# The first products after two inner norms run on unnormalised activations, with rstd and the shift applied to their sums

## The chip, the cores and the metric

The kernel runs on one core of one Trainium2 chip. The metric is the device time of one execution in microseconds (us), taken as the median of several runs; lower is better. TensorE (PE in the profile) multiplies matrices, VectorE (DVE), ScalarE (ACT) and GpSimd (POOL) do elementwise work, and SyncE (SP) issues the transfers from HBM. Each engine works through its own queue in order and waits on semaphores for the others.

## The reference

One decoder layer for 256 tokens of width 2048, all in float32. Each of three sublayers first normalises x and modulates it with a scale and a shift computed from a condition c:

```python
def ada_in(x, g, shift, scale):
    y = rmsnorm(x, g) * (1.0 + scale[:, None, :]) + shift[:, None, :]
    return y
...
    mod = cond @ ada_w[l] + ada_b[l]
    sh1, sc1, gt1, sh2, sc2, gt2, sh3, sc3, gt3 = jnp.split(mod, N_MOD, axis=-1)
    h = ada_in(x, norm_g[l, 0], sh1, sc1)
    x = x + MACARON_W * gt1[:, None, :] * swiglu(h, ffn_w_gate[l, 0], ffn_w_up[l, 0], ffn_w_down[l, 0])
    h = ada_in(x, norm_g[l, 1], sh2, sc2)
    x = x + gt2[:, None, :] * hybrid_mixer(h, ...)
    h = ada_in(x, norm_g[l, 2], sh3, sc3)
    x = x + MACARON_W * gt3[:, None, :] * swiglu(h, ffn_w_gate[l, 1], ffn_w_up[l, 1], ffn_w_down[l, 1])
return rmsnorm(x, final_norm)
```

rmsnorm divides each token's vector by the root of its mean square: one factor rstd for each token. swiglu has 5632 hidden units (44 tiles of 128, called f). hybrid_mixer projects h to eight heads of forgetting attention (q, k, v), to q, k, v, z of eight heads of a gated delta rule, and to 24 gate rows; the delta rule's q, k and v go through a causal convolution of four taps and a silu, and its keys into a triangular solve.

## The kernel before

x lies feature-major in SBUF, as 16 blocks j (or k) of 128 features by 256 tokens. The weights stream from HBM in blocks of eight 128x128 tiles (512 KB). For each block `Stream.next` (L85 to L106) issues a DMA into `wraw`, has ScalarE cast the high half `whi` (L95) and VectorE subtract it to get the low half `wlo` (L98, the "low split"); three buffers of each rotate, and a fourth during the ffns. Both operands of every product are so split in two, and three partial products stand for one float32 product. `mm` (L360) does a tile in two matmuls: the high weights on high and low activations side by side (512 columns), the low weights on the high activations (256 columns). The mixer's `project` uses three matmuls of 256 columns (L614 to L616).

The modulated activations are `hs`, [128, 16, 2, 256], high and low beside each other for each k. The columns of `mod` (shift, scale and gate of the three sublayers) are computed along the way: `ada_col` (L193) loads 1 MB and reduces it on VectorE (L214, tile `adat`). The table `RATE` says how many of them go with each weight block; `W.quiet` stops them for the last three j of an ffn's second half.

The stages run one after another: ffn0, the mixer, ffn1, the final norm. An ffn runs in two halves of its f tiles; each half computes gate and up products (`pg`, `pu`, summed over k), silu and product (`hid`), and then for each of the 16 blocks j the down products `pd`. `residual` (L385, L386) adds a block's sum to x, in two VectorE steps: one for each half of the 512 columns, scaled by the gate column `gh` (L383). In the second half `sumsq_add` squares the new block on ScalarE (`sq`, L257) and adds it up on GpSimd (`sqacc`, L261). The mixer ends in the out projection, which does the same with sums called `po`: four blocks at once, then one after the other.

The norm stands between two stages. `norm_rstd` sums the squares over the partitions (`nsum`, L269), takes root and reciprocal in small steps (L274 to L279), and spreads rstd into a row that lies on all partitions (`rb` L283, `nrow` L284). Then `modulate_one` makes a block of `hs`: x times g(1 + scale) times the row (`ht`, L297), plus the shift, rounded to the high half on ScalarE and subtracted to the low half on VectorE (L299 to L304). `h_need(k)` has four blocks made ahead of the product that reads block k. ffn1 starts with a group of two f (four sums) that runs over k in the outer loop; the mixer's first stage has the gate rows `gt` and three key heads (four sums), also with k outside.

In the mixer, `ORDER` sets the sequence of the projections: K is a key head, Z and V rows for four heads at once (`project_rows`, L627 to L629), G a delta-rule head's q and v, F an attention head. Convolutions (`cv`, L763 to L765), gates (L656 to L698) and the solve are generators whose steps are taken between product tiles, and `finish` forces what a later step needs. Within the order in which the program is written, a scheduler places the instructions of each engine.

## Time and profile before

| | us |
|---|---|
| median of 3 runs | 2083.11 |
| lowest, highest run | 2080.29, 2083.84 |
| the profiled execution | 2078.41 |
| its span in the trace | 2076.6 |
| VectorE, low splits (674 of 1228 ns) | 823.6 |
| ScalarE, casts of the high halves (674 of 1048 ns) | 701.8 |
| VectorE, ada columns (140 of 2352 ns) | 329.3 |

The mean clock that TensorE was granted in the profiled execution is 0.988. A row of a timeline reads: start and duration, engine, line, operation, output from inputs, shape, count; a bracket at its end gives the idle time of that engine before it, and what ended it. A row of a group reads: line, engine, operation, names, shapes and count, then busy time and the mean of one in ns, then the idle time before them and what ended it. Several matmuls are in flight at once, so a matmul's own duration is longer than the distance to the next.

### The profile page before, as it was taken

The numbers are of one execution on the slowest core, as the hardware profiler recorded it, in microseconds if no ns is written. First come the engines' busy times: TensorE is split into PE (matmuls) and PEld (weight loads), VectorE is DVE, ScalarE is ACT, GpSimd is POOL, SyncE is SP. The second block draws the span as 40 slices with busy tenths as digits, with TensorE's granted clock in tenths as the row PEclk, the third lists the DMA queues.
The fourth block names the chain that finished last, engine by engine and source line by source line (L and its number), as shares of the span: only waits on it lengthen the run. The fifth ranks groups of instructions, "written<-read, shape, count | busy, mean of one in ns | idle before, by whom it ended". The sixth has DMA issues, their size and how long they took to land.

```text
span 2076.6 us, 33353 instructions
## 1 busy us (share of the span) xinstructions
PE 2029.3 (98%) x12965; PEld 1825.4 (88%) x12966; DVE 1559.8 (75%) x2386; ACT 1012.5 (49%) x1577; POOL 66.8 (3%) x60
## 2 busy tenths in 40 slices
...
GB/s 312 349 326 323 279 208 255 360 339 368 333 328 326 330 304 182 236 251 231 206 258 224 197 241 281 205 231 231 240 234 213 185 190 184 191 184 189 187 184 110
DMA packets 129488, 519.55 MB, mean 250 GB/s; under 512 B 18217, under 2 KB 21545, under 8 KB 111153
## 3 DMA queue, kind: packets, MB, share of 16 engines
...
q8 instruction: 102, 1.67, 0.3%
...
## 4 chain that ended last, share of the span: by engine, by line
PE 87%; DVE 6%; DMA 2%; ACT 2%; issue 1%; DVEq 0%; SPq 0%; ACTq 0%
PE pd L361 15%; PE pu L361 11%; PE pg L361 11%; PE pd L362 8%; PE pg L362 5%; PE pu L362 5%; PE pgu L431 5%; PE pgu L429 5%; PE pgu L430 5%; PE po L361 3%; PE pp L614 2%; PE pp L616 2%; PE pp L615 2%; DVE wlo L98 2%; PE po L362 1%
## 5 line engine op out<-in xcount | busy, mean ns | idle before, releaser
L98 DVE TENSOR_TENSOR wlo<-wraw,whi 128x1024 fp32r<-128x1024 f32 x674 | 823.6, 1228 | 348.7 <-ACT whi L95 346.4
L95 ACT CAST whi<-wraw 128x1024 fp32r<-128x1024 f32 x674 | 701.8, 1048 | 685.5 <-issue 171.0
L361 PE MATMUL pd<-hid,whi 128*128 128x512 f32 x1408 | 497.0, 397 | 0.0
L362 PE MATMUL pd<-hid,wlo 128*128 128x256 f32 x1408 | 396.0, 281 | 0.8 <-DVE wlo L98 0.7
L361 PE MATMUL pg<-hs,whi 128*128 128x512 f32 x960 | 342.5, 397 | 2.3 <-DVE hs L304 1.8
L361 PE MATMUL pu<-hs,whi 128*128 128x512 f32 x960 | 343.2, 398 | 0.0
L214 DVE CUSTOM_DVE_ANT_0 adat<-adat,cs,colt 128x2048 f32<-128x2048 f32 x140 | 329.3, 2352 | 16.5 <-DMA adat<-in_ada_dram 16.1
L361 PEld LDWEIGHTS pd<-hid,whi 128*128 128x128 f32 x1408 | 264.2, 188 | 64.7
L362 PE MATMUL pg<-hs,wlo 128*128 128x256 f32 x960 | 270.6, 282 | 0.0
L362 PE MATMUL pu<-hs,wlo 128*128 128x256 f32 x960 | 270.2, 281 | 0.0
L362 PEld LDWEIGHTS pd<-hid,wlo 128*128 128x128 f32 x1408 | 265.4, 189 | 2.5 <-DVE wlo L98 2.1
L429 PE MATMUL pgu<-hs,whi 128*128 128x256 f32 x896 | 251.4, 283 | 5.2 <-ACT hs L300 4.0
L431 PE MATMUL pgu<-hs,wlo 128*128 128x256 f32 x896 | 250.7, 284 | 2.4 <-DVE wlo L98 2.3
L430 PE MATMUL pgu<-hs,whi 128*128 128x256 f32 x896 | 252.2, 283 | 0.0
L361 PEld LDWEIGHTS pg<-hs,whi 128*128 128x128 f32 x960 | 181.0, 188 | 45.8 <-issue 2.1
L361 PEld LDWEIGHTS pu<-hs,whi 128*128 128x128 f32 x960 | 180.9, 188 | 43.9
L614 PE MATMUL pp<-hs,whi 128*128 128x256 f32 x656 | 191.9, 294 | 4.0 <-ACT whi L95 2.1
L616 PE MATMUL pp<-hs,wlo 128*128 128x256 f32 x656 | 188.9, 289 | 0.5 <-DVE wlo L98 0.4
L615 PE MATMUL pp<-hs,whi 128*128 128x256 f32 x656 | 188.3, 287 | 0.0
L362 PEld LDWEIGHTS pg<-hs,wlo 128*128 128x128 f32 x960 | 181.9, 190 | 0.0
L362 PEld LDWEIGHTS pu<-hs,wlo 128*128 128x128 f32 x960 | 181.9, 189 | 0.0
L429 PEld LDWEIGHTS pgu<-hs,whi 128*128 128x128 f32 x896 | 171.0, 192 | 6.3 <-ACT hs L300 4.4
...
## 6 DMA issues: line engine op xcount, KB each, us to landing
wraw<-in_w_dram SPq DMA_DIRECT2D x674, 512.0 KB, 4.2
adat<-in_ada_dram SPq DMA_DIRECT2D x140, 1024.0 KB, 6.6
...
```

The source lines that it names most:

```text
L95: nc.scalar.copy(self.h, r)
L98: nc.vector.tensor_tensor(self.l, r, self.h.bitcast(F32), ALU.subtract)
L214: V.tensor_tensor_reduce(t, t, cs, 1.0, L("adab", q, 1), ALU.mult, ALU.add, mod[:, q : q + 1])
L361: PE.matmul(ps, wt[0], act.rearrange("p a t -> p (a t)"), start=first, stop=False)
L362: PE.matmul(ps[:, :T], wt[1], act[:, 0], start=False, stop=last)
L429: PE.matmul(o, wh, hs[:, k, 0], start=first and s == 0, stop=False, skip_group_check=skip)
L430: PE.matmul(o, wh, hs[:, k, 1], start=False, stop=False, skip_group_check=skip)
L431: PE.matmul(o, wl, hs[:, k, 0], start=False, stop=last, skip_group_check=skip)
L614: PE.matmul(pp[i][:, :T], wh, hs[:, k, 0], start=(k == 0), stop=False)
L615: PE.matmul(pp[i][:, :T], wh, hs[:, k, 1], start=False, stop=False)
L616: PE.matmul(pp[i][:, :T], wl, hs[:, k, 0], start=False, stop=(k == KD - 1))
```

## The change

Since rstd is one factor for each token, it can be multiplied into a product's sum after the fact: W(x g (1 + scale) rstd + shift) = rstd W(x g (1 + scale)) + W shift.

- `hs` gets a flat layout of 514 columns for each k: low half, high half, and two columns with the high and low half of the shift.
- A class `Early` stands for a norm. `y(j)`, called after each residual of ffn0's second half and of the out projection, takes the gain g(1 + scale) of block j (`g1`, VectorE), writes its product with x as the high half (ScalarE, L334) and the low half (VectorE, L335). `norm1` is that of the mixer, `norm2` that of ffn1.
- `products` does a tile in three matmuls: the high weights on the high half and the shift (258 columns), the high weights on the low half (256), the low weights on the high half and the shift (258).
- `step(k)` puts the sum of the squares at k = 2 and the row at k = 4 of the first products; the row is copied to SBUF. From then on `modulate_one` writes the finished blocks over `hs`, behind the products that read it.
- `scaled` finishes a sum: the two shift columns are added, the sum is multiplied by the row, and the shift's product is handed on as a bias for the next step.
- The mixer's first stage now holds the gate rows and five key heads (six sums), ffn1's first group three f (six sums). `ORDER` has V0 ahead of G0, and V0 finishes the chain of keys up to head 0.
- `W.quiet` and the rules that held VectorE's low splits and ada columns behind the norm (`W.held`, `W.hold` from `norm_rstd`) are gone.
- Products on finished blocks use `mm_h`, the same two matmuls as `mm`.

```diff
+N_EARLY = 5
...
-ORDER = ("K3 K4 K5 K6 K7 Z0 G0 V0 F0 G1 F1 G2 F2 G3 F3 V1 Z1 G4 F4 G5 F5 G6 G7 F6 F7").split()
+ORDER = ("K5 K6 K7 Z0 V0 G0 F0 G1 F1 G2 F2 G3 F3 V1 Z1 G4 F4 G5 F5 G6 G7 F6 F7").split()
...
-    def norm_rstd(keep_row=False):
+    def norm_sums():
...
+        for t in range(2):
+            V.tensor_scalar(rb[:, t], L("ones"), y[:, t : t + 1], None, ALU.mult)
+        return rb
+    def norm_row(rb, eng):
         pr = psf("nrow")
         for t in range(2):
-            last = V.tensor_scalar(rb[:, t], L("ones"), y[:, t : t + 1], None, ALU.mult)
             PE.matmul(pr[:, t * P : (t + 1) * P], rb[:, t], ident, start=True, stop=True)
-        W.held = ([None, sqa["hold"]] if sqa["hold"] is not None else []) + [last.ins]
-        if not keep_row:
-            return pr[:, :T]
         row = tmp.tile([P, T], F32, name="nrow", bufs=1)
-        V.tensor_copy(row, pr[:, :T])
+        eng(row, pr[:, :T])
         return row
-    hs = keep.tile([P, KD, 2, T], F32R, name="hs")
+    hs = keep.tile([P, KD, 2 * T + 2], F32R, name="hs")
+    LO, HI, HIS, ALL = slice(0, T), slice(T, 2 * T), slice(T, 2 * T + 2), slice(0, 2 * T)
...
-    def modulate(which, m_sh, m_sc):
-        ada_need(max(m_sh, m_sc), KD - 1)
-        g1 = gains(which, m_sc, 0, KD)
-        r = norm_rstd()
-        hq["next"], hq["one"] = 0, lambda j: modulate_one(
-            j, g1[:, j : j + 1], mod[:, m_sh * KD + j : m_sh * KD + j + 1], r)
+    class Early:
+        def __init__(self, which, m_sh, m_sc):
+            self.which, self.m_sh, self.m_sc, self.row, self.sums = which, m_sh, m_sc, None, None
+        def y(self, j):
+            ada_need(self.m_sc, j)
+            ada_need(self.m_sh, KD - 1)
+            if j == 0:
+                sh = mod[:, self.m_sh * KD : (self.m_sh + 1) * KD]
+                A.copy(hs[:, :, 2 * T], sh)
+                V.tensor_sub(hs[:, :, 2 * T + 1], sh, hs[:, :, 2 * T].bitcast(F32))
+            g = gains(self.which, self.m_sc, j, 1)
+            A.activation(hs[:, j, HI], x[:, j], AF.Copy, scale=g)
+            V.scalar_tensor_tensor(hs[:, j, LO], x[:, j], g, hs[:, j, HI].bitcast(F32), ALU.mult, ALU.subtract)
+        def step(self, k):
+            if k == 2:
+                self.sums = norm_sums()
+            if k == 4:
+                self.row = norm_row(self.sums, A.copy)
+                g1 = gains(self.which, self.m_sc, 0, KD)
+                hq["next"], hq["one"] = 0, lambda j: modulate_one(
+                    j, g1[:, j : j + 1], mod[:, self.m_sh * KD + j : self.m_sh * KD + j + 1], self.row)
+            if k > 4:
+                h_upto(min(k, k - 4 + max(0, k - 10)))
+        def products(self, ps, wt, k):
+            PE.matmul(ps[:, : T + 2], wt[0], hs[:, k, HIS], start=(k == 0), stop=False)
+            PE.matmul(ps[:, :T], wt[0], hs[:, k, LO], start=False, stop=False)
+            PE.matmul(ps[:, : T + 2], wt[1], hs[:, k, HIS], start=False, stop=(k == KD - 1))
+        def scaled(self, dst, ps, rows=slice(0, P)):
+            s = tiny.tile([P, 2], F32, name="shc", tag="shc", bufs=8)
+            A.copy(s[rows, :1], ps[rows, T : T + 1])
+            V.tensor_add(s[rows, 1:], ps[rows, T + 1 : T + 2], s[rows, :1])
+            V.tensor_tensor(dst, ps[rows, :T], self.row[rows], ALU.mult)
+            return s[rows, 1:]
...
-        while hq["next"] < min(KD, k + AHEAD):
+        h_upto(k + AHEAD)
+    def h_upto(n):
+        while hq["next"] < min(KD, n):
...
+    def mm_h(ps, wt, k):
+        PE.matmul(ps, wt[0], hs[:, k, ALL], start=(k == 0), stop=False)
+        PE.matmul(ps[:, T:], wt[1], hs[:, k, HI], start=False, stop=(k == KD - 1))
...
+            first = early is not None and len(grp) > 1
+            for i, (f, m, k) in enumerate(todo):
+                if first:
+                    if i % (2 * len(grp)) == 0:
+                        early.step(k)
+                    early.products(pg[f, m], W.next((m, which), k, f), k)
+                else:
+                    h_need(k)
+                    mm_h(pg[f, m], W.next((m, which), k, f), k)
...
+                if first:
+                    sg, su = early.scaled(tg, pg[f, "g"]), early.scaled(tu, pg[f, "u"])
+                    A.activation(tg, tg, AF.Silu, bias=sg)
+                    V.scalar_tensor_tensor(tu, tu, su, tg, ALU.add, ALU.mult)
+                    hd = hp.tile([P, 2, T], F32R, name="hid", tag="hid")
+                    split(hd, tu)
+                    hids.append(hd)
...
-                    if half == 0:
-                        modulate(2 * which, m_sh, m_sc)
-                    hids = gate_up(which, part, 2 if half == 0 else 1, hp)
+                    hids = gate_up(which, part, 3 if half == 0 else 1, hp, early if half == 0 else None)
...
                     if half == 1:
                         sumsq_add(j)
-                        if j == KD - 4:
-                            W.quiet = True
+                        if after is not None:
+                            after.y(j)
                         if j == KD // 2:
                             sqrt_table(x[:, j, :1])
-                W.quiet = False
...
+    norm1, norm2 = Early(1, 3, 4), Early(2, 6, 7)
     if dbg is None or "ffn1" in dbg:
-        ffn(0, 0, 1, 2)
+        ffn(0, 2, None, norm1)
...
         def gates(ps):
             yr = x[:, 8]
-            A.copy(yr[R], ps[R])
+            sh = norm1.scaled(yr[R], ps, R)
+            A.activation(yr[R], yr[R], AF.Identity, bias=sh)
...
-                if h:
-                    finish("k", NH)
+                finish("k", NH if h else 0)
...
-        first = project([("gt", 0)] + [("qkv", NH + h) for h in range(3)])
-        start("k", -1, gates(first[0]))
-        for h in range(3):
-            have_keys(h, first[1 + h])
+        first = [("gt", 0)] + [("qkv", NH + h) for h in range(N_EARLY)]
+        pp = [psn(i, "pp") for i in range(len(first))]
+        for k in range(KD):
+            norm1.step(k)
+            for i, (m, n) in enumerate(first):
+                norm1.products(pp[i], W.next(m, k, n), k)
+        h_upto(KD)
+        start("k", -1, gates(pp[0]))
+        for h in range(N_EARLY):
+            v = pt("v")
+            sh = norm1.scaled(v, pp[1 + h])
+            A.activation(v, v, AF.Identity, bias=sh)
+            have_keys(h, v)
...
                 residual(pj[q], j, 5, False)
                 sumsq_add(j)
+                norm2.y(j)
...
-        ffn(1, 6, 7, 8)
+        ffn(1, 8, norm2)
```

Three places show how instructions move. The first is TensorE at norm 1, between the last down product of ffn0 (`pd`) and the first of the mixer (`pp`). Before:

```order
L362 MATMUL pd_8121<-hid_7307,wlo_8147 128x256
L269 MATMUL nsum_8177<-colt_87,sqacc_7362 128x2 [waits Pool_49]
L269 MATMUL nsum_8177<-colt_87,sqacc_7362 128x2
L269 MATMUL nsum_8177<-colt_87,sq_8170 128x2 [waits Activation_49]
L269 MATMUL nsum_8177<-colt_87,sq_8170 128x2
L284 MATMUL nrow_8192<-colt_87,rb_8191 128x128 [waits DVE_49] x2
L614 MATMUL pp_8245<-hs_126,whi_8269 128x256 [waits PE_49,Activation_49]
L614 MATMUL pp_8246<-hs_126,whi_8269 128x256 [waits PE_49]
L614 MATMUL pp_8247<-hs_126,whi_8269 128x256 [waits PE_49]
```

After:

```order
L411 MATMUL pd_8186<-hid_7307,wlo_8215 128x256
L270 MATMUL nsum_8349<-colt_87,sqacc_7362 128x2 [waits Pool_49]
L270 MATMUL nsum_8349<-colt_87,sqacc_7362 128x2
L270 MATMUL nsum_8349<-colt_87,sq_8238 128x2 [waits Activation_49]
L270 MATMUL nsum_8349<-colt_87,sq_8238 128x2
L350 MATMUL pp_8295<-hs_126,whi_8303 128x258 [waits Activation_49]
L351 MATMUL pp_8295<-hs_126,whi_8303 128x256
L350 MATMUL pp_8296<-hs_126,whi_8303 128x258 [waits DVE_49,PE_49]
L351 MATMUL pp_8296<-hs_126,whi_8303 128x256
```

and some rows on:

```order
L351 MATMUL pp_8298<-hs_126,whi_8303 128x256
L350 MATMUL pp_8299<-hs_126,whi_8303 128x258
L351 MATMUL pp_8299<-hs_126,whi_8303 128x256
L350 MATMUL pp_8300<-hs_126,whi_8303 128x258
L352 MATMUL pp_8295<-hs_126,wlo_8304 128x258 [waits DVE_49]
```

The row's two matmuls have left this place; the first product waits for ScalarE alone, and the high weights of the first block go to five sums twice and to the sixth once before a low weight is used. The row stands 72 products later.

The second place is TensorE at norm 2, from the last product of the out projection (`po`) on; before, the sum and the row stood directly behind it, as at norm 1. After, there come first the products, then behind 36 of them the sum,

```order
L411 MATMUL po_14324<-oh_13573,wlo_14350 128x256
L350 MATMUL pg_14391<-hs_126,whi_14399 128x258 [waits Activation_49]
L351 MATMUL pg_14391<-hs_126,whi_14399 128x256
L352 MATMUL pg_14391<-hs_126,wlo_14400 128x258 [waits DVE_49]
L350 MATMUL pu_14392<-hs_126,whi_14399 128x258 [waits DVE_49,PE_49]
```

```order
L352 MATMUL pu_14396<-hs_126,wlo_14430 128x258
L270 MATMUL nsum_14445<-colt_87,sqacc_13675 128x2 [waits Pool_49]
L270 MATMUL nsum_14445<-colt_87,sqacc_13675 128x2
L270 MATMUL nsum_14445<-colt_87,sq_14371 128x2 [waits Activation_49]
L270 MATMUL nsum_14445<-colt_87,sq_14371 128x2
```

and behind 36 more the row:

```order
L352 MATMUL pu_14396<-hs_126,wlo_14477 128x258
L290 MATMUL nrow_14504<-colt_87,rb_14459 128x128 [waits DVE_49] x2
L350 MATMUL pg_14391<-hs_126,whi_14513 128x258
L351 MATMUL pg_14391<-hs_126,whi_14513 128x256
L352 MATMUL pg_14391<-hs_126,wlo_14514 128x258
```

What stood between `po` and `pg` stands between products now.

The third place is VectorE in the down products of ffn0's second half, from one residual to the next but one. Before:

```order
L385 SCALAR_TENSOR_TENSOR x_85<-pd_7581,gh_7626,x_85 128x256
L98 TENSOR_TENSOR wlo_7662<-wraw_7659,whi_7661 128x1024
L386 SCALAR_TENSOR_TENSOR x_85<-pd_7581,gh_7626,x_85 128x256
L98 TENSOR_TENSOR wlo_7692<-wraw_7689,whi_7691 128x1024
L383 TENSOR_SCALAR gh_7736<-mod_125 128x1
L98 TENSOR_TENSOR wlo_7714<-wraw_7711,whi_7713 128x1024
L385 SCALAR_TENSOR_TENSOR x_85<-pd_7633,gh_7681,x_85 128x256
L386 SCALAR_TENSOR_TENSOR x_85<-pd_7633,gh_7681,x_85 128x256
L214 ISA adat_7717,mod_125<-adat_7717,cs_86,colt_87 128x2048
L214 ISA mod_125 128x1
L383 TENSOR_SCALAR gh_7791<-mod_125 128x1
L98 TENSOR_TENSOR wlo_7747<-wraw_7744,whi_7746 128x1024
```

After:

```order
L434 SCALAR_TENSOR_TENSOR x_85<-pd_7603,gh_7648,x_85 128x256
L99 TENSOR_TENSOR wlo_7688<-wraw_7685,whi_7687 128x1024
L435 SCALAR_TENSOR_TENSOR x_85<-pd_7603,gh_7648,x_85 128x256
L99 TENSOR_TENSOR wlo_7722<-wraw_7719,whi_7721 128x1024
L335 SCALAR_TENSOR_TENSOR hs_126<-x_85,g1_7655,hs_126 128x256
L432 TENSOR_SCALAR gh_7766<-mod_125 128x1
L315 SCALAR_TENSOR_TENSOR g1_7773<-mod_125,colt_87 128x1
L99 TENSOR_TENSOR wlo_7744<-wraw_7741,whi_7743 128x1024
L434 SCALAR_TENSOR_TENSOR x_85<-pd_7659,gh_7707,x_85 128x256
L435 SCALAR_TENSOR_TENSOR x_85<-pd_7659,gh_7707,x_85 128x256
L215 ISA adat_7747,mod_125<-adat_7747,cs_86,colt_87 128x2048
L215 ISA mod_125 128x1
```

For each block there is one step more on `hs` and one more on `g1`, with ada column and low splits around them.

Behind the end of the mixer's first stage VectorE now begins with the convolutions of five key heads and their six scalings, where it had the convolutions of three. Up to the low split of Z0's first block those of K0 to K5 stand there in both kernels; the step that starts the solve's matrix (`Ln`, from `cstt`) and most of K6's convolution, which stood ahead of that split, come behind it.

43 lines of the change are left out of this document (20 added, 23 removed).

## Prediction

> **What bounds the kernel now.** I began with the page's first two lists, which give the busy share of each engine over the whole span, and then the chain that ended last.
>
> ```profile
> span 2076.6 us, 33353 instructions
> PE 2029.3 (98%) x12965; PEld 1825.4 (88%) x12966; DVE 1559.8 (75%) x2386; ACT 1012.5 (49%) x1577; POOL 66.8 (3%) x60
> PE 87%; DVE 6%; DMA 2%; ACT 2%; issue 1%; DVEq 0%; SPq 0%; ACTq 0%
> ```
>
> TensorE is busy for 98% of the span, so the kernel is bound by matmuls, and what can be won is the time in which TensorE stands or runs at half clock. The profiled execution took 2078.41 us, 1.8 above its span; the median of the runs shown is 2083.11, 4.7 above that execution. Differences worked out below from the trace are taken off the median.
>
> The next view is the timeline around the second inner norm (before ffn1). These are TensorE's rows from the last product of the out projection to the first of ffn1.
>
> ```profile
> 1305.89 0.28 PE L362 MATMUL po<-oh,wlo 128*128 128x256 f32 x1
> 1306.01 0.57 PE L269 MATMUL nsum<-colt,sqacc 128*128 128x2 f32 x4
> ...
> 1307.77 0.61 PE L269 MATMUL nsum<-colt,sq 128*128 128x2 f32 x4 [1.19 <-ACT sq L257]
> ...
> 1309.91 1.22 PE L284 MATMUL nrow<-colt,rb 128*128 128x128 f32 x4 [1.53 <-DVE rb L283]
> ...
> 1312.98 0.76 PE L361 MATMUL pg<-hs,whi 128*128 128x512 f32 x1 [1.84 <-DVE hs L304]
> ```
>
> Each bracket is a wait for another engine: the square of the last block, the rstd row, the first modulated block. From 1306.17 to 1312.98 no product runs: 6.81 us. The first norm (before the mixer) has the same shape:
>
> ```profile
> 787.66 0.28 PE L362 MATMUL pd<-hid,wlo 128*128 128x256 f32 x1
> ...
> 789.08 0.42 ACT L257 ACTIVATE sq<-x 128x256 f32<-128x256 f32 x1 [1.99 <-DVE x L386]
> ...
> 791.68 0.71 PE L284 MATMUL nrow<-colt,rb 128*128 128x128 f32 x4 [1.53 <-DVE rb L283]
> ...
> 793.95 1.22 PE L614 MATMUL pp<-hs,whi 128*128 128x256 f32 x4 [1.55 <-ACT hs L303]
> ```
>
> From 787.94 to 793.95 it is 6.01 us. A table of windows shows that the gaps cost more than their length (columns: window, length, busy time of each engine with its count, then granted clock, DMA share and GB/s):
>
> ```profile
> 200.00:320.00 120.00, 120.00 (x1009) 120.00 (x1008) 98.07 (x148) 59.02 (x86) 0.00 (x0) 1.00 0.71 250
> 787.70:794.00 6.30, 1.96 (x15) 1.59 (x13) 5.47 (x14) 1.29 (x4) 1.32 (x5) 0.93 0.59 209
> 794.00:800.00 6.00, 6.00 (x28) 6.00 (x29) 4.35 (x12) 3.13 (x7) 0.42 (x2) 0.51 0.27 87
> 800.00:802.00 2.00, 2.00 (x19) 2.00 (x18) 1.67 (x3) 2.00 (x6) 0.00 (x0) 1.00 0.00 0
> 1313.00:1319.00 6.00, 6.00 (x19) 5.13 (x20) 4.78 (x11) 2.93 (x6) 0.00 (x0) 0.52 0.16 54
> 1400.00:1700.00 300.00, 300.00 (x1705) 261.12 (x1704) 186.26 (x233) 130.49 (x170) 0.00 (x0) 1.00 0.63 216
> ```
>
> For some 6 us after each gap the clock is 0.51 and 0.52. At full clock a 256-column matmul takes 120/1009 = 0.119 us, and a pair of 512 and 256 columns takes 300/852.5 = 0.352. So 28 matmuls in 6.00 us instead of 28 x 0.119 = 3.33 lose 2.67 at norm 1, and 9.5 pairs instead of 3.34 lose 2.66 at norm 2. The two norms cost 8.7 and 9.5 us, and 18.2 us is the most that the change can recover.
>
> **Norm 2, part by part.** The gains g(1 + scale) are now applied behind each residual of the out projection, so when the last product ends only the last block or two of hs are missing, and k = 0 of ffn1's first group (3 f, six sums) starts at once. The order shows 12 tiles (36 matmuls) ahead of the eight small matmuls of the sum, and another 12 ahead of the row's. The 6.81 us go and with them the half clock (2.66). What comes in: the sum's and row's matmuls now stand between products, 0.57 + 0.61 + 0.71 = 1.9 (the row at norm 1's price, where the clock had not yet dropped). A tile costs three matmuls, 0.357, instead of a pair, 0.352: over 96 tiles 0.5. Two more columns in two matmuls of a tile are 2 x 0.119 x 2/256 x 96 = 0.2. One sum of the six waits for a bank that a residual still reads; it is put behind others in the order, 0.1. That is 9.47 - 2.7 = **6.8 won**. No row shows 258 columns or hs rows of this stride. The nearest are 256 columns at 0.119 and 512 at 2 x 0.352/3 = 0.235 (the pair's 768 columns are three times 256); at the upper end the two wide matmuls of 192 tiles would cost 2 x 0.116 x 192 = 45 us. I take the line between them, 0.120, since twice the columns take twice the time in these rows; the far end is left to the cases outside the range.
>
> **Norm 1.** The small sum still stands ahead of the first product, because the last block of x is needed first. In before, the first three casts of the mixer's weights were done ahead of the gap; now ScalarE's order is square, HI copy of block 15, then the first cast. From these rows:
>
> ```profile
> L95 ACT CAST whi<-wraw 128x1024 fp32r<-128x1024 f32 x31 | 32.0, 1051 | 27.5 <-PE pp L615 9.7 <-DMA wraw<-in_w_dram 8.4 <-DVE x L819 5.0
> L300 ACT CAST hs<-ht 128x256 fp32r<-128x256 f32 x8 | 3.2, 397 | 0.1
> ```
>
> the square ends at 789.50, the copy at 789.90, the cast at 790.95: the first product stands at about 791.15, 3.2 us after the last pd instead of 6.01. Its low-weight matmuls need one split more (1.22), but the order puts eleven high-weight ones (1.3 us) in front. Minus 0.7 for the row inline and 0.2 for the columns, TensorE wins 1.9 here, or 4.6 if the half clock goes too: the gap is then 3.2 with 0.6 of work in it. In norm 1 of before the row's matmuls at +3.7 us were still at full clock (0.71), in norm 2 they were not (1.22); so either can happen.
>
> The Trainium skill ("TensorE: Matmul & The Clock Gate", Part 1) says that the clock halves after a whole idle window of some 3.4 us and returns after about as long of work. By that rule a gap of 3.2 us would never halve it. The row at norm 2 speaks against it being as simple: it was slow 3.7 us after the last product though sums had run in between.
>
> **The mixer's start** decides what becomes of it. Where TensorE's first Z0 product and its first low split stood before:
>
> ```profile
> 787.94:852.50 64.56, 59.77 (x469) 58.15 (x468) 53.23 (x120) 45.29 (x87) 1.75 (x7) 0.95 0.55 191
> 851.29 1.21 DVE L98 TENSOR_TENSOR wlo<-wraw,whi 128x1024 fp32r<-128x1024 f32 x1
> 855.62 0.40 PE L627 MATMUL pv<-whi,hs 128*128 128x512 f32 x1
> L765 DVE SCALAR_TENSOR_TENSOR cv<-pp,colt,cv 128x255 f32<-128x255 f32 x8 | 3.6, 465 | 0.0
> L301 DVE TENSOR_TENSOR hs<-ht,hs 128x256 fp32r<-128x256 f32 x8 | 3.4, 421 | 0.9 <-ACT hs L300 0.9
> L672 DVE SCALAR_TENSOR_TENSOR x<-x 128x48 f32<-128x48 f32 x7 | 1.4, 201 | 0.1
> L747 DVE TENSOR_TENSOR Ln<-cstt,x 128x1024 f32<-128x1024 f32 x1 | 1.2, 1222 | 0.0
> L214 DVE CUSTOM_DVE_ANT_0 adat<-adat,cs,colt 128x2048 f32<-128x2048 f32 x2 | 4.7, 2350 | 1.2 <-DMA adat<-in_ada_dram 1.2
> ```
>
> DVE was busy 53.2 of the 64.6 us to that split, and TensorE came to Z0 67.7 us after the last pd. Now the first stage holds five key heads and not three, so their convolutions begin only at 3.2 + 96 x 0.357 + 0.7 = 38.2. Between that point and Z0's first low split the order has on DVE 18 convolution steps (8.4), six scalings (0.42 + 0.15 each, 3.4), some six splits (7.3), two ada columns (4.7), about twenty-five small steps of the gates (5) and the last of h (1): 30 us. TensorE has K5 to K7 in that time, 48 x 0.357 = 17.1, and the gates' and keys' small matmuls. If DVE starts on this only at 38.2, Z0 begins at 68, as before, and all is eaten: 0. If it clears its h work early, 4.6 stay. The step that starts the solve's matrix (1.2) and most of K6's convolution (0.9) are moved behind that split; if all that hangs on them comes later by twice as much and is waited for, -4. I take **+2.5**, the middle of 0 and 4.6, since V0's products (96 of 512 columns, 22.5 us) now stand ahead of G0, which needs the keys.
>
> **The tail of ffn0.** Here the new work meets a loaded DVE:
>
> ```profile
> 697.50:787.70 90.20, 90.20 (x513) 78.31 (x513) 77.99 (x99) 40.08 (x52) 21.98 (x14) 1.00 0.82 306
> 702.00:774.00 72.00, 72.00 (x410) 62.53 (x409) 66.96 (x83) 30.35 (x41) 19.06 (x12) 1.00 0.81 305
> 774.00:787.70 13.70, 13.70 (x80) 11.89 (x79) 7.08 (x11) 6.31 (x8) 2.93 (x3) 1.00 0.80 283
> L386 DVE SCALAR_TENSOR_TENSOR x<-pd,gh,x 128x256 f32<-128x256 f32 x15 | 7.2, 480 | 0.2
> L383 DVE TENSOR_SCALAR gh<-mod 128x1 f32<-128x1 f32 x14 | 2.1, 148 | 0.0
> L214 DVE CUSTOM_DVE_ANT_0 adat<-adat,cs,colt 128x2048 f32<-128x2048 f32 x10 | 24.3, 2428 | 0.0
> ```
>
> DVE is busy 78.0 of 90.2. Added: sixteen LO halves, of the residual's form (0.48, 7.7), sixteen gains (0.148, 2.4), and, since the quiet stretch of the last three blocks is gone, two more ada columns (2.43 each, 4.9). That is 93.0 in 90.2, so TensorE must wait for low splits by about 2.8. The lead of a split is a whole block j at times, which may hide all of it (0); orders in which a residual waits for its pd and splits stand behind it may double it (-6). I take **-2.5**.
>
> **The out projection** is the same at a lower load:
>
> ```profile
> 1237.00:1305.00 68.00, 66.95 (x378) 57.96 (x379) 53.89 (x63) 31.51 (x40) 18.19 (x14) 1.00 0.74 279
> ```
>
> 53.9 plus thirteen times 0.63 (8.2) is 62 of 68: it fits, with a burst of four blocks at its start; bounds 0 and -2, taken **-0.7**. ScalarE, at 30 to 40 of 90 us, takes one 0.4 us copy for each block without a wait of its own.
>
> Sum: 6.8 + 2.5 - 2.5 - 0.7 = 6.1 us off, 2083.1 - 6.1 = **2077.0** (the profiled execution would be 2072.3, its span 2070.5).
>
> **Rivals.** (a) DVE keeps up everywhere and both gaps go with their slow clock: 6.8 + 4.6 = 11.4, 2071.7. For it speaks that TensorE did not wait once in 702 to 774 with DVE at 93%; against it, 93.0 in 90.2. (b) Only the clock of norm 1 differs from the forecast: a 3.2 us gap does not halve it, and DVE lets 2.1 more through: 2074.9. This is what the gate's rule in the Trainium skill page named above gives. (c) DVE is the bound at the mixer's start: all of norm 1 eaten and the moved work waited for, 6.8 - 4 - 2.5 - 0.7 = -0.4, 2083.5, no change. (d) The other side: in ffn0's tail each LO half waits on DVE for ScalarE's HI copy, which stands behind a cast (1.05) and a square (0.42), and the splits behind it come late. With 1 us of wait in each of 16, DVE needs 78.0 + 16 x 1.63 + 4.9 = 109.0 for 90.2: -18.8, in all -10.2 and 2093.3. It makes the kernel slower by 0.2% once a wait passes 0.63 us. Against it: in the order a split or an ada column stands between most residuals and their LO half, which gives ScalarE 1.2 to 2.4 us.
>
> **How the numbers follow.** A measurement of this kernel tells some 0.2% (4.2 us) from no change. Chances: the forecast 0.36, (a) 0.20, (b) 0.10, (c) 0.16, (d) 0.13, something unseen 0.05. The forecast's own spread reaches past 4.2 us won in three quarters of it: faster 0.27 + 0.30 = 0.57; same 0.09 + 0.16 and a part of the unseen, 0.26; slower 0.17. The range goes from 3.7 below (a), where a loss put down to DVE is smaller than any bound here, to 5.5 above (c), which takes the weaker half of (d): 2068 to 2089. The cases that win have a range of their own, 2070 to 2079.
>
> **What would show it.** At norm 2 the first product follows the last po within 0.5 us, and the clock stays at 1.00 over the next 6 us; if it stands, the HI copy or the cast is late. At norm 1 the first product comes near 3.2 us after the last pd. In ffn0's tail TensorE's waits for low splits sum to 2 to 3 us; over 6 is (d). At the mixer's start, Z0's first product stands 63 to 66 us after the last pd, not 67.7; if it is later, (c). A matmul of 258 columns above 0.125 us would break every term.

## The result, and the profile after

| | before | the change |
|---|---|---|
| median of 6 runs each | 2082.28 us | 2089.66 us |
| lowest to highest | 2078.71 to 2084.62 | 2086.49 to 2090.25 |
| the profiled execution, its span | 2078.41, 2076.6 | 2090.25, 2088.5 |

The ratio is 1.0035, with a 95% interval of 1.0023 to 1.0047: the change makes the kernel 7.4 us slower. The two profiled executions are 11.9 us apart by their spans, since that of before lies below all its six runs and that of the change is the slowest of its six; the accounts below are made between these two, so a part of what they show as lost, some 4.5 us, is no loss of the usual run.

The page of the changed kernel reads at first like that of before, and its chain of waits shows where to look: VectorE's share went from 6% to 8%, "issue" from 1% to 3%.

```profile
span 2088.5 us, 33744 instructions
PE 2036.9 (98%) x13062; PEld 1837.3 (88%) x13062; DVE 1580.4 (76%) x2470; ACT 1029.7 (49%) x1627; POOL 68.0 (3%) x60
PE 82%; DVE 8%; issue 3%; DMA 3%; ACT 2%; DVEq 0%; SPq 0%; ACTq 0%
```

A table of windows, cut at the stages' first and last products, tells more. In order: ffn0's tail (down products of its second half), from the last pd to Z0, from Z0 to the out projection, the out projection. Before:

```profile
697.43:787.94 90.51, 90.51 (x517) 78.62 (x515) 78.06 (x99) 40.08 (x52) 21.98 (x14) 1.00 0.82 306
787.94:855.62 67.68, 62.89 (x496) 61.27 (x494) 55.62 (x128) 48.40 (x94) 1.75 (x7) 0.95 0.56 193
855.62:1209.40 353.78, 346.92 (x2509) 322.42 (x2508) 294.07 (x698) 218.14 (x461) 0.43 (x2) 1.00 0.65 226
1209.40:1306.17 96.77, 94.20 (x537) 80.90 (x535) 74.99 (x114) 46.12 (x70) 19.78 (x14) 1.00 0.72 271
```

The changed kernel:

```profile
697.72:790.91 93.19, 91.69 (x517) 78.58 (x515) 89.92 (x131) 42.92 (x64) 22.08 (x14) 1.00 0.84 311
790.91:860.49 69.58, 63.13 (x479) 61.23 (x478) 56.70 (x124) 49.36 (x84) 1.74 (x7) 0.91 0.56 197
860.49:1226.34 365.85, 354.79 (x2524) 329.53 (x2524) 295.91 (x723) 226.76 (x491) 0.43 (x2) 0.98 0.62 219
1226.34:1324.22 97.88, 94.61 (x537) 80.94 (x536) 87.02 (x144) 51.52 (x84) 20.40 (x14) 1.00 0.76 287
```

The tail lost 2.7 us, with VectorE busy 89.9 of 93.2 instead of 78.1 of 90.5. The out projection lost 1.1. The stretch between them, from ffn0's last product to the out projection, went from 421.5 to 435.4: 14.0 lost, most of it behind Z0. TensorE's idle time in it (length less busy time) went from 4.8 + 6.9 to 6.5 + 11.1 us, 5.9 more. The rest is the clock: 0.95 and 1.00 became 0.91 and 0.98. By the records of the granted clock TensorE was busy at half clock for 23.8 us instead of 6.0. Half of that is lost against full clock: 11.9 us instead of 3.0, which is 8.9 more. The busy time, counted at full clock, is the same within 1 us.

Norm 2 did what the change says. From the last product of the out projection TensorE goes straight on, one sum waits 0.46 us for a residual, and the sum of the squares stands 36 products later. The second fence is the window of the first 8 us, at full clock.

```profile
1323.94 0.28 PE L411 MATMUL po<-oh,wlo 128*128 128x256 f32 x1
1324.06 0.28 PE L350 MATMUL pg<-hs,whi 128*128 128x258 f32 x1
...
1327.08 0.36 PE L350 MATMUL pg<-hs,whi 128*128 128x258 f32 x1 [0.46 <-DVE x L435]
...
1329.07 0.50 PE L270 MATMUL nsum<-colt,sqacc 128*128 128x2 f32 x4
1329.43 0.59 PE L270 MATMUL nsum<-colt,sq 128*128 128x2 f32 x4
```

```profile
1324.06:1332.00 7.94, 7.48 (x63) 7.31 (x62) 6.82 (x16) 3.87 (x7) 0.66 (x1) 1.00 0.59 191
```

From the last po to the first down product of ffn1 it takes 251.3 us instead of 257.9: 6.6 won. At norm 1 the gap shrank from 6.0 to 2.9 us. Square, HI copy and the first cast follow one another on ScalarE, and the clock still falls behind them (the second fence is the window of the 6 us from the first product on):

```profile
792.04 0.42 ACT L258 ACTIVATE sq<-x 128x256 f32<-128x256 f32 x1 [2.74 <-DVE x L435]
...
792.37 0.49 ACT L334 ACTIVATE hs<-x,g 128x256 fp32r<-128x256 f32 x1
...
792.76 1.03 ACT L96 CAST whi<-wraw 128x1024 fp32r<-128x1024 f32 x1
...
793.85 0.58 PE L350 MATMUL pp<-hs,whi 128*128 128x258 f32 x1 [0.73 <-ACT whi L96]
```

```profile
793.85:800.00 6.15, 6.15 (x29) 6.15 (x30) 4.66 (x10) 2.90 (x4) 0.00 (x0) 0.51 0.84 275
```

New is a standstill ahead of Z0. K7's last product ends at 850.1; then come the gates' matmuls (`prow`, L750), which wait for the last of a chain of small steps on VectorE and ScalarE, with an ada column and table loads (`ACT_TABLE_LOAD`, the row that stands ahead of a change of ScalarE's function) in between:

```profile
849.22 1.28 ACT L724 ACT_TABLE_LOAD   x1
...
851.06 2.34 DVE L215 CUSTOM_DVE_ANT_0 adat<-adat,cs,colt 128x2048 f32<-128x2048 f32 x1
851.17 1.28 ACT L827 ACT_TABLE_LOAD   x1
...
854.12 0.20 DVE L737 TENSOR_TENSOR x<-x,coef 128x48 f32<-128x48 f32 x1
...
854.37 0.56 PE L750 MATMUL prow<-cstt,x 128*8 128x128 f32 x2 [3.39 <-DVE x L737]
```

```profile
850.10:860.50 10.40, 6.25 (x33) 4.94 (x31) 6.62 (x21) 6.70 (x13) 0.00 (x0) 0.71 0.01 2
860.50:868.00 7.50, 6.68 (x17) 5.11 (x18) 7.42 (x17) 6.39 (x17) 0.00 (x0) 0.50 0.66 220
```

No weight arrives in these 10 us (DMA share 0.01): SyncE issues none from 844.6 to 862.0. In its queue the store of the gates' row (`rowd`) comes first, and it waits 12.7 us for the gates' matmuls by way of ScalarE; then the next weight waits for a low split to free its buffer. The row gives who waited for whom, us in total, times, longest us:

```profile
SPq L762 <- ACT x L761: 12.7, 1, 12.7
```

With the gates written first (e9 below) this wait is 0.9 us; how much of the loss it makes is not shown. The clock halves, and Z0's first 7.5 us run at 0.50. In the kernel before the gates' matmuls stood between products without a wait, and their last one (`pcum`) ended 51 us after the last pd; in the change it ended after 69 us, just ahead of Z0. The first two rows are of before, the third of the change:

```profile
836.43 0.39 PE L689 MATMUL prow<-cstt,x 128*8 128x128 f32 x2
838.98 0.37 PE L698 MATMUL pcum<-x,colt 128*128 128x8 f32 x2
859.15 0.57 PE L759 MATMUL pcum<-x,colt 128*128 128x8 f32 x2
```

A second stretch at half clock, 6.83 us from 970.5 on, follows a wait of 2.07 us for the silu of a q behind Z0:

```profile
969.60 0.33 PE L918 MATMUL pvq<-colt,qv 128*128 128x128 f32 x1 [2.07 <-ACT qv L827]
```

### The profile page after: what moved, and what is told of

Its sections match the earlier page's. It is cut to its first block, busy times and chain, and to the rows that moved or that the text cites. A ratio compares the mean times of both kernels' runs of the same rounds, so it can differ in the third digit from the quotient of the medians.

```text
span 2088.5 us, 33744 instructions
## 1 busy us (share of the span) xinstructions
PE 2036.9 (98%) x13062; PEld 1837.3 (88%) x13062; DVE 1580.4 (76%) x2470; ACT 1029.7 (49%) x1627; POOL 68.0 (3%) x60
## 4 chain that ended last, share of the span: by engine, by line
PE 82%; DVE 8%; issue 3%; DMA 3%; ACT 2%; DVEq 0%; SPq 0%; ACTq 0%
PE pd L410 13%; PE pu L406 10%; PE pg L406 10%; PE pd L411 7%; PE pu L407 5%; PE pg L407 5%; PE pgu L494 4%; PE pgu L492 4%; PE pgu L493 4%; DVE wlo L99 3%; PE pp L676 2%; PE pp L674 2%; PE pp L675 2%; DMA adat<-in_ada_dram 1%; DVE adat L215 1%
## 5 line engine op out<-in xcount | busy, mean ns | idle before, releaser
L406 PE MATMUL pu<-hs,whi 128*128 128x512 f32 x912 | 324.6, 396 | 0.0
L406 PE MATMUL pg<-hs,whi 128*128 128x512 f32 x912 | 323.3, 395 | 0.3 <-DVE shc L358 0.3
L407 PE MATMUL pu<-hs,wlo 128*128 128x256 f32 x912 | 257.6, 282 | 0.0
L407 PE MATMUL pg<-hs,wlo 128*128 128x256 f32 x912 | 256.4, 281 | 0.0
L406 PEld LDWEIGHTS pg<-hs,whi 128*128 128x128 f32 x912 | 171.6, 188 | 40.4 <-ACT shc L357 0.5
L406 PEld LDWEIGHTS pu<-hs,whi 128*128 128x128 f32 x912 | 171.8, 188 | 39.9
L492 PEld LDWEIGHTS pgu<-hs,whi 128*128 128x128 f32 x896 | 169.1, 189 | 6.6 <-ACT hs L305 4.5
L407 PEld LDWEIGHTS pg<-hs,wlo 128*128 128x128 f32 x912 | 172.8, 189 | 0.0
L494 PEld LDWEIGHTS pgu<-hs,wlo 128*128 128x128 f32 x896 | 168.0, 189 | 3.6 <-DVE wlo L99 3.4
L493 PEld LDWEIGHTS pgu<-hs,whi 128*128 128x128 f32 x896 | 169.4, 189 | 0.3 <-DVE hs L306 0.2
L674 PE MATMUL pp<-hs,whi 128*128 128x256 f32 x560 | 165.1, 295 | 0.3 <-DVE shc L358 0.3
```

The source lines that it names most:

```text
L406: PE.matmul(ps, wt[0], hs[:, k, ALL], start=(k == 0), stop=False)
L407: PE.matmul(ps[:, T:], wt[1], hs[:, k, HI], start=False, stop=(k == KD - 1))
L492: PE.matmul(o, wh, hs[:, k, HI], start=first and s == 0, stop=False, skip_group_check=skip)
L493: PE.matmul(o, wh, hs[:, k, LO], start=False, stop=False, skip_group_check=skip)
L494: PE.matmul(o, wl, hs[:, k, HI], start=False, stop=last, skip_group_check=skip)
L674: PE.matmul(pp[i][:, :T], wh, hs[:, k, HI], start=(k == 0), stop=False)
```

## The experiments

All ratios are to the kernel before, run on the same chip, with 95% intervals. The change itself was measured once, in the comparison above. The stretches come from one profiled execution of each kernel: tail (first to last pd of ffn0's second half), gap (last pd to first product of the mixer, by start of the one and modelled end of the other), to Z0, Z0 to the out projection, the out projection, and from there to ffn1's down products. "Gates" is the time from ffn0's last product to the end of the gates' last matmul (`pcum`). Four pairs of kernels below differ in the out projection alone (e11 and e14, e10 and e16, e6 and e17, e9 and e18). Within them the stretches ahead of it differ by up to 2.8 us, and their sum from the last pd on by up to 2.6, so smaller differences between two rows tell little.

| kernel | ratio | tail | gap | to Z0 | Z0 to out | out | norm 2 and up | gates |
|---|---|---|---|---|---|---|---|---|
| before | 1 | 90.5 | 6.0 | 61.7 | 353.8 | 96.8 | 257.9 | 51 |
| the change | 1.0035 (1.0023 to 1.0047) | 93.2 | 2.9 | 66.6 | 365.8 | 97.9 | 251.3 | 69 |
| e1 three heads | 0.9994 (0.9982 to 1.0006) | 93.1 | 2.9 | 69.6 | 347.4 | 99.1 | 251.5 | 48 |
| e2 Z0 G0 V0 | 1.0015 (1.0005 to 1.0024) | 93.2 | 2.9 | 66.6 | 357.4 | 99.0 | 252.4 | 69 |
| e3 norm 2 alone | 0.9993 (0.9984 to 1.0002) | 90.5 | 8.2 | 61.5 | 355.8 | 97.5 | 251.3 | 52 |
| e4 no ada columns | 1.0049 (1.0030 to 1.0068) | 93.2 | 2.9 | 74.8 | 353.8 | 100.8 | 252.9 | 63 |
| e5 quiet | 1.0015 (1.0006 to 1.0025) | 92.8 | none | 64.2 | 359.7 | 99.7 | 251.6 | 62 |
| e6 three heads, Z0 G0 V0 | 0.9989 (0.9980 to 0.9999) | 93.2 | 2.9 | 69.5 | 347.8 | 98.8 | 251.6 | 48 |
| e9 gates first | 0.9989 (0.9980 to 0.9998) | 93.2 | 2.9 | 66.1 | 353.3 | 97.3 | 251.5 | 59 |
| e10 norm 2 alone, hold | 0.9999 (0.9990 to 1.0008) | 90.5 | 6.1 | 60.6 | 354.0 | 101.0 | 251.4 | 50 |
| e11 quiet, gates first | 0.9993 (0.9982 to 1.0004) | 92.8 | none | 58.7 | 361.2 | 99.7 | 251.5 | 52 |
| e12 quiet, three heads, Z0 G0 V0 | 1.0003 (0.9993 to 1.0014) | 92.8 | none | 66.0 | 354.4 | 99.5 | 251.7 | 46 |
| e13 quiet, three heads, gates first | 1.0019 (1.0008 to 1.0030) | 92.8 | none | 66.7 | 358.5 | 99.2 | 251.8 | 48 |
| e14 e11, late halves | 0.9994 (0.9984 to 1.0005) | 92.8 | none | 59.7 | 362.6 | 97.7 | 251.9 | 52 |
| e15 e11, row early | 1.0004 (0.9995 to 1.0014) | 92.8 | none | 58.9 | 362.2 | 100.5 | 251.4 | 52 |
| e16 e10, late halves | 0.9986 (0.9977 to 0.9996) | 90.5 | 6.0 | 61.2 | 354.8 | 98.8 | 251.4 | 51 |
| e17 e6, late halves | 0.9982 (0.9972 to 0.9991) | 93.2 | 2.9 | 70.6 | 346.2 | 95.3 | 255.8 | 50 |
| e18 e9, late halves | 0.9996 (0.9987 to 1.0006) | 93.2 | 2.9 | 66.0 | 356.1 | 96.0 | 252.2 | 59 |
| e19 e14, no ada columns | 0.9985 (0.9971 to 0.9998) | 92.8 | none | 59.1 | 355.2 | 98.4 | 254.6 | 52 |
| e20 e14, Z0 G0 V0 | 1.0004 (0.9992 to 1.0016) | 92.8 | none | 58.8 | 363.7 | 99.1 | 251.6 | 52 |

**Which part of the change costs.** Theories: the late bunch (a first stage of six sums lets gates and five convolutions come late and at once), the order (V0 ahead of G0), and throughput (VectorE has more work than time).

e1, three key heads in the first stage:

```diff
-N_EARLY = 5
-ORDER = ("K5 K6 K7 Z0 V0 G0 F0 ...
+N_EARLY = 3
+ORDER = ("K3 K4 K5 K6 K7 Z0 V0 G0 F0 ...
```

> First stage with three key heads and not five (K3 and K4 as own projections behind it again); V0 stays ahead of G0, all else as in the change. Late bunch (the gates' chain and five convolutions reach VectorE together after a longer first stage, and TensorE's gate matmuls stand still ahead of Z0): 8 or more of the 14 us that the mixer lost come back, about 2081. Order (V0 ahead of G0 is what costs): within 2 us of the change, 2088 to 2091. Throughput (VectorE simply has more work than time in the mixer's start): two scalings fewer, 1 us, 2088 to 2089.

e2, V0 behind G0 again:

```diff
-ORDER = ("K5 K6 K7 Z0 V0 G0 F0 ...
+ORDER = ("K5 K6 K7 Z0 G0 V0 F0 ...
...
-                finish("k", NH if h else 0)
+                if h:
+                    finish("k", NH)
```

> Z0 G0 V0 again instead of Z0 V0 G0, and V0 finishes no keys; five key heads in the first stage stay. Order: most of what is lost behind Z0's start (about 9 us of the 14) comes back, 2080 to 2083. Late bunch: the standstill ahead of Z0 is untouched, 2087 to 2092; since G0 needs the keys of heads 0 to 3 at once, it may be slower than the change. Throughput: no change, 2089.

e4, no ada columns at the mixer's start (in `RATE`, columns for each weight block from the given block on):

```diff
-... (264, 0.1), (280, 0.25), ...
+... (264, 0.0), (300, 0.31), ...
```

> As the change, but no ada columns with the mixer's first 36 weight blocks (they are made up in the blocks behind, 0.31 for each). Three columns of 2.35 us leave VectorE's queue ahead of Z0's second low split. Throughput: 5 to 7 us come back, 2083 to 2085. Late bunch: the one column that stands between the gates' steps (2.3 us) counts, 2087. Order: 2089.

Three heads give back all that the change had lost, e2 about half, e4 nothing. In e1 TensorE comes to Z0 later than in the change, 72.5 us after the last pd instead of 69.6, and is done with the rest 18 us sooner:

```profile
793.44:865.97 72.53, 63.22 (x493) 61.08 (x494) 62.56 (x147) 59.07 (x116) 1.75 (x7) 0.95 0.58 203
865.97:1213.35 347.38, 345.42 (x2509) 322.68 (x2508) 290.63 (x696) 211.95 (x452) 0.43 (x2) 1.00 0.64 228
```

What differs ahead of Z0 is that the gates' matmuls end at 48 us and not at 69, and that VectorE was busy 62.6 us and not 56.7: it waited less. Behind Z0 TensorE idles 2.0 us instead of 11.1, and the clock stays at 1.00. A part of what e1 and e6 give back at norm 1 is not theirs: their gap there is the same 2.9 us, but no half clock followed it, which cost the change 3 us. Behind Z0, V0's place costs 8 us with five heads and nothing with three (e6 against e1), so it is not a cause by itself. Throughput falls as the reason of the standstill: e4 took columns out of it, and it grew; TensorE waits 5.8 us there for one cast. Behind Z0 the same kernel takes 353.8 us, 12.0 less than the change, so columns seem to count there; the sum to the out projection is 431.5 instead of 435.4, and 4.5 are lost again up to ffn1's down products.

e6, both of e1 and e2 together:

> Norm 1 and norm 2 early, three key heads in the first stage and Z0 G0 V0: the change without the two changes of sequence. If five key heads alone make the loss and V0's place costs only together with them: as with three key heads alone, ratio 0.999. If V0's place costs by itself some 4 us: ratio 0.997.

The first case held within the interval (e1 0.9994, e6 0.9989).

**The gates' chain itself.** e9 keeps five heads and V0's place, and only writes the gates' steps ahead:

```diff
         start("k", -1, gates(pp[0]))
+        advance("k")
+        advance("k")
         for h in range(N_EARLY):
```

> As the change (five key heads, V0 ahead of G0), but the gates' steps up to the decay rates are written ahead of the five scalings and convolutions, so that VectorE and ScalarE get them first and the gates' Exp no longer alternates with the convolutions' Silu. Nothing is computed less. Late gates (TensorE stands ahead of Z0 because the gates' chain is stretched by what lies between its steps): the standstill of 10.4 us ahead of Z0 and the half clock behind it go, 10 or more of the 14 us come back, ratio to before 0.998 to 1.000. Late keys (the convolutions themselves come too late with five heads): they come later still, the standstill stays or moves to V0, ratio 1.003 or more.

The time came back, 0.9989, but not quite as expected. Z0 begins as late as in the change (69.0 us), with two waits of 2 us for a key head in front of it; what is gone is the loss behind it. The groups on ScalarE from 832 to 861 us show what lay between the gates' steps: the rows load a table each time that ScalarE goes from the gates' Exp to the convolutions' Silu. In the change:

```profile
L827 ACT ACT_TABLE_LOAD x4 | 5.1, 1283 | 0.1
...
L711 ACT ACT_TABLE_LOAD x1 | 1.3, 1283 | 0.0
L722 ACT ACT_TABLE_LOAD x1 | 1.3, 1283 | 0.0
```

With the gates first L827, the convolutions' Silu, needs only half as many:

```profile
L827 ACT ACT_TABLE_LOAD x2 | 2.6, 1283 | 0.0
```

and in the 10.45 us ahead of Z0 VectorE and ScalarE are busy 10.0 each instead of 6.6 and 6.7 of 10.4: there they are now full, and in the change they waited for each other.

```profile
850.00:860.45 10.45, 6.37 (x48) 5.70 (x48) 9.99 (x20) 10.02 (x31) 0.00 (x0) 0.91 0.58 206
```

From the last pd to Z0 ScalarE loads 4 tables instead of 7; what of the gain comes from fewer loads and what from the shorter way through the queues is not shown.

**Norm 1's gap.** e5 brings back the quiet last blocks of ffn0 (and of ffn1):

```diff
                     if half == 1:
                         sumsq_add(j)
+                        if j == KD - 4:
+                            W.quiet = True
                         if after is not None:
                             after.y(j)
...
+                W.quiet = False
```

> As the change, but no ada columns in the last three blocks of ffn0's second half, as before. Loaded VectorE in the tail: of the 2.7 us that the tail lost, about 1 to 2.7 come back in its stretch of the trace (90.5 to 92 us instead of 93.2); ratio 1.002 to 1.003. If the tail's loss comes from the LO halves and not from the columns: 93 us again, ratio 1.0035. The stretch ahead of Z0 is not touched by either.

The tail hardly changed (93.2 to 92.8), so its loss is not in the two columns. Four products in the change's tail stand 0.49 to 0.96 us behind the one before them. Three of them (at 726, 749 and 773) lie ahead of the last three blocks and are in e5 too; only the fourth, at 787.6, is gone. From 702 to 774 us VectorE is full in the change, busy 71.2 of 72.0 us instead of 67.0, and its costliest new step is the LO half:

```profile
702.00:774.00 72.00, 70.59 (x396) 60.48 (x396) 71.15 (x103) 34.50 (x51) 19.05 (x11) 1.00 0.84 318
L335 DVE SCALAR_TENSOR_TENSOR hs<-x,g,hs 128x256 fp32r<-128x256 f32 x15 | 13.7, 912 | 0.9 <-ACT hs L334 0.9
```

What changed in e5 was norm 1. ScalarE's queue now has two casts (at 788.01) ahead of the last block's square (at 792.80), where the change has its first cast behind square and HI copy (at 792.76). So the weights are ready in time, the first product follows the last pd without a gap, and the sum stands 36 products later, as at norm 2:

```profile
788.01 1.98 ACT L96 CAST whi<-wraw 128x1024 fp32r<-128x1024 f32 x2
...
790.99 0.28 PE L411 MATMUL pd<-hid,wlo 128*128 128x256 f32 x1
791.11 0.28 PE L350 MATMUL pp<-hs,whi 128*128 128x258 f32 x1
...
792.80 0.42 ACT L258 ACTIVATE sq<-x 128x256 f32<-128x256 f32 x1 [2.81 <-DVE x L435]
...
795.42 0.51 PE L270 MATMUL nsum<-colt,sqacc 128*128 128x2 f32 x4
```

So the quiet blocks that the change dropped were what its early form needed at norm 1. Why the scheduler puts the casts first without the columns is not shown.

**Norm 2 alone.** e3 makes the mixer's norm as before:

```diff
-        ffn(0, 2, None, norm1)
+        ffn(0, 2, None, None)
...
+        modulate(1, 3, 4)
...
-        pp = [psn(i, "pp") for i in range(len(first))]
-        for k in range(KD):
-            norm1.step(k)
...
+        pp = project(first)
         start("k", -1, gates(pp[0]))
         for h in range(N_EARLY):
-            v = pt("v")
-            sh = norm1.scaled(v, pp[1 + h])
-            A.activation(v, v, AF.Identity, bias=sh)
-            have_keys(h, v)
+            have_keys(h, pp[1 + h])
```

with three heads, Z0 G0 V0 and unscaled sums.

> Only norm 2 is early; the mixer's norm is made as before (row first, then finished blocks), with three key heads and Z0 G0 V0; the rule that held low splits behind the norm is not restored. If the parts add up as in the trace (norm 2 wins 6.6, the out projection loses 1.1, the rest belongs to norm 1): 2082.3 - 5.5 = 2077, faster than both. If norm 2's gain needs norm 1's early form or is lost again behind: 2082 or more.

Norm 2's 6.6 us are there, but its gap at norm 1 is 2.2 us longer than before, and 2 us were lost behind Z0, which is within the spread named above. e10 restores the rule on low splits (`W.held` with the residual's and the row's last steps) and the quiet blocks:

> Only norm 2 early, as in the earlier run, but with the rule that keeps low splits behind norm 1's row steps restored, and the quiet last blocks of ffn0. The gap at norm 1 was 8.2 us without the rule and 6.0 with it in the kernel before: 2.2 us come back, ratio 0.9975 (some 5 us faster than before). If the rule was not the reason: 0.999 as in the earlier run.

The gap is back at 6.1 (the rule and the quiet blocks came back together, so which of them did it is not told), yet the ratio is 0.9999: the out projection took 101.0 us. Its four first blocks end together; each now hands ScalarE a HI copy, and the casts stand behind them. In e11, which has the same burst, TensorE waits 2.38 us there for one cast (and loses 3.0 us in that stretch to the half clock):

```profile
1239.72 0.49 ACT L334 ACTIVATE hs<-x,g 128x256 fp32r<-128x256 f32 x1
...
1240.43 0.49 ACT L334 ACTIVATE hs<-x,g 128x256 fp32r<-128x256 f32 x1
...
1241.29 1.03 ACT L96 CAST whi<-wraw 128x1024 fp32r<-128x1024 f32 x1
...
1242.37 0.57 PE L410 MATMUL po<-oh,whi 128*128 128x512 f32 x1 [2.38 <-ACT whi L96]
```

**Both causes removed.** e11 is e5 with e9, e12 is e5 with e6, e13 is e5 with e1 and e9.

> As the change, with the quiet last blocks of ffn0 and the gates' steps ahead of the convolutions. If the two causes are separate (the ada columns hold up ScalarE's cast and so the first product at norm 1; what lies between the gates' steps holds up TensorE ahead of Z0): the gap at norm 1 goes to 0.2 us without half clock behind it (5 to 6 us better than gates first alone), ratio to before 0.995 to 0.9965. If the time won at norm 1 is only waited for at the gates, since VectorE and ScalarE are the bound of the mixer's start: as gates first alone, 0.999.

> Quiet blocks, three key heads in the first stage and Z0 G0 V0: the mixer's sequence of before with norm 1 early. It had no gap at Z0 without the quiet blocks, but waits of 9 us within the first stage and K3 to K7. Separate causes: ratio 0.996 to 0.9975. Bound in the mixer's start by VectorE and ScalarE: 0.999, as without the quiet blocks.

> Quiet blocks, three key heads, gates first and V0 ahead of G0: all that has been seen to help. Separate causes: the best, 0.995 to 0.996. Bound by VectorE and ScalarE in the mixer's start: no better than 0.998.

The causes are not separate; no sum of gains appeared, and e13, which has all that had helped by itself and was expected to be the best, is slower than before. Its trace has waits of 3.1 and 2.4 us ahead of Z0 and 425.2 us up to the out projection; why was not followed up. In e11 the gap is gone and TensorE is at Z0 after 58.7 us, 9 us ahead of before, with 0.4 us idle and no half clock:

```profile
793.46:852.20 58.74, 58.32 (x483) 57.27 (x481) 51.43 (x122) 43.58 (x84) 1.75 (x7) 1.00 0.62 212
852.20:1213.37 361.17, 351.49 (x2521) 325.35 (x2520) 300.21 (x721) 220.33 (x482) 0.42 (x2) 1.00 0.64 224
```

and gives 7.4 of them back behind it. From the last pd to the out projection it takes 419.9 us, as in e1 (419.9), e6 (420.2) and e12 (420.3), and before 421.5; by the pairs named above these are not told apart.

**The burst.** e14 is e11 with the halves of the first four blocks made later; e16, e17 and e18 do the same to e10, e6 and e9.

```diff
-                norm2.y(j)
+                if 4 <= j < 8:
+                    norm2.y(j - 4)
+                if j >= 4:
+                    norm2.y(j)
```

> As quiet blocks with gates first, and norm 2's halves of the out projection's first four blocks are made with blocks 4 to 7 and not in one burst. The out projection lost 0.6 to 4 us in the early kernels, with three waits of 3 us in sum behind the burst, in some runs at half clock. Burst: its stretch is back at 97 us, 1 to 2 us better than without. If the burst is not the reason: the same waits and the same stretch.

> Norm 2 alone early, norm 1 as in the kernel before with quiet blocks and its rule for low splits, and the halves of the out projection's first four blocks made with blocks 4 to 7. Burst: the out projection takes 97 to 98 us and not 101, and norm 2's 6.5 us remain: some 5 to 6 us faster than before, ratio 0.997 to 0.9975. Otherwise as without the late halves, 0.9999.

> Both norms early with three key heads and Z0 G0 V0 (0.9989 before), with the late halves in the out projection. Burst: 1 to 2 us better, 0.998 to 0.9985. Otherwise 0.999.

> The change with the gates first (0.9989 before) and the late halves in the out projection. It had no half clock in the out projection and took only 0.6 us more there than the kernel before, so little is left to win: 0.9985 to 0.999 by either theory.

The stretch fell by 2.0, 2.2, 3.5 and 1.3 us, the same way in all four. The ratios do not confirm it: each interval overlaps that of the kernel without the late halves, and e18's is no lower than e9's. e16 and e17 are faster than before by 1.4 and 1.8 in a thousand, as e6, e9 and e19 are by 1.1 to 1.5; e14 and e18 are not told from before. In e17's profiled execution the stretch behind it is 4.2 us longer than in e6's (255.8 against 251.6): TensorE waits there 1.84 us for the last block's residual, which stands behind an ada column and two low splits on VectorE, and 6.83 us at half clock follow.

**What bounds the 420 us.** e15 is e11 with the row at norm 1 made after two steps instead of four, and finished blocks made up to k at once:

```diff
-            if k == 2:
+            a, b = (1, 2) if self.which == 1 else (2, 4)
+            if k == a:
...
-            if k == 4:
+            if k == b:
...
-            if k > 4:
-                h_upto(min(k, k - 4 + max(0, k - 10)))
+            if k > b:
+                h_upto(k if self.which == 1 else min(k, k - 4 + max(0, k - 10)))
```

> Quiet blocks and gates first, and at norm 1 the squares are summed at k = 1 and the row made at k = 2 of the first products (not 2 and 4), with finished blocks made up to k at once (not k - 4). Put-off h work (VectorE idles while it waits for the row and is full afterwards): VectorE's first 20 us fill (13 to 15 us busy become 16 or more) and the stretch to the out projection falls from 419.9 to 414 to 417, ratio 0.997 to 0.998. If the bound lies behind Z0 in the solve: 419 to 421 as before it, ratio 0.999 to 1.000.

VectorE's first 20 us filled from 14.9 to 16.7 busy, and nothing was won: 421.1. Two more take the amount of work and the sequence apart, by the edits of e4 and e2 on e14:

> Quiet blocks, gates first, late halves in the out projection (0.9994 before), and no ada columns with the mixer's first 36 weight blocks. Amount of work: three columns of 2.35 us leave the stretch in which VectorE is full, 3 to 6 us come back, ratio 0.9965 to 0.998. Sequence of waits: 0.999 to 1.000, since the columns lay in VectorE's idle time; what is put off may cost a little later.

> Quiet blocks, gates first, late halves, and Z0 G0 V0 as in the kernel before. Sequence: G0 wants the keys of heads 0 to 3 22 us earlier; if V0's place is what costs behind Z0, the stretch from Z0 to the out projection falls from 361 to 354 to 357 us, ratio 0.997 to 0.998. Amount of work: no change, 0.999 to 1.000.

The sequence changed nothing (363.7 behind Z0, 362.6 in e14): V0's place, which cost 8 us with the gates at 69, costs nothing with them at 52. In e19 the stretch behind Z0 fell to 355.2 and the sum to 414.3 (422.4 in e14, 419.9 in e11), with the clock at 1.00 throughout:

```profile
789.73:848.84 59.11, 58.44 (x484) 57.23 (x482) 49.07 (x122) 43.50 (x84) 1.75 (x7) 1.00 0.54 180
848.84:1204.04 355.20, 348.27 (x2517) 323.95 (x2518) 296.46 (x713) 225.82 (x484) 0.43 (x2) 1.00 0.65 226
```

The edit moves columns more than it removes them: up to the out projection there are 25 instead of 26, but none up to 58 us behind Z0, where e14 has six. So what is shown is that VectorE's work at the mixer's start counts, and there not its amount over the whole stretch. In e4 the same edit shortened the stretch behind Z0 too, but the standstill ahead of it grew. In time, e19's 0.9985 and e14's 0.9994 have intervals that overlap, and e19's profiled execution is the fastest of its ten, 2.8 us below their median, so this rests on single executions.

## Why the prediction was wrong

- Norm 2, 6.8 won: right, 6.6. The 258-column matmul costs what a 256-column one does (0.12 us from start to start in the rows of norm 2), and the small matmuls fit between products.
- Norm 1, first product 3.2 us after the last pd: right, 2.9. Whether the half clock stays was left open; it stayed in the change (0.51). Rival (b), by which a gap of that length does not halve the clock, is half true: of the eight kernels with this gap, six had half clock behind it, and e1 and e6 had none. What the prediction did not ask is why the cast came late; it took it as given by the order. It was the dropped quiet stretch (e5).
- The tail, 2.5 lost: 2.7, with VectorE's load as the reason, but by terms that were off both ways, so the closeness is in part luck. The two columns, priced at 4.9 of work, cost 0.4 (e5). The LO halves took 0.91 us each and not 0.48, 13.7 in all, while the low splits beside them became cheaper (31 in 37.6 us instead of 32 in 41.9). VectorE's busy time grew by 11.9 us where the sum had 15.0. Rival (d) fell: a LO half waited for ScalarE only once in the tail, for 0.9 us.
- The out projection, 0.7 lost: 1.1 in the change, within its bounds. The burst of the first four blocks has a part in it; making their halves later gave back 1.3 to 3.5 in four other kernels, 2.2 of the 4.2 that e10 had lost.
- **The mixer's start, 2.5 won with bounds of -4 and 4.6: this step failed.** 14.0 were lost from ffn0's last product to the out projection. The sum asked when TensorE reaches Z0, found 63 to 68 us, and took that as the price (with 2.5 for the middle of 0 and 4.6, which is 2.3); it was 69.6, not far off the bad end. But arriving at Z0 is worth nothing by itself: e1 arrives 5 us later than before and is 6.4 us faster behind it, e11 arrives 9 us earlier and is 7.4 slower. What counts is how far the gates and keys have come, and those the changed order moved back by 18 us (69 against 51); with the gates' steps first (e9) or with three heads (e1) the loss is gone. The sum had put the gates' 25 small steps at 5 us of VectorE's time, as work. They are a chain across VectorE, ScalarE and TensorE, and between its links lay convolutions, a column and table loads; TensorE's gate matmuls then stood in its queue ahead of Z0. The threshold that the prediction named (Z0 later than 67.7) pointed to rival (c). It was near in that moved work came late and was waited for, but its reason, VectorE as the bound, was not so (VectorE idled 12.9 of the 69.6 us), and its price of 4 was too small.
- The second half of the miss is the clock. The prediction counted half clock at the norms and nowhere else; the new standstills were followed by 13.65 and 6.83 us of it, and half clock took 8.9 of the 14 us, idle time the rest.

The measured 2089.66 lies just above the range, whose end came from (c) with part of (d).

What stays open: why the time that e11 wins at norm 1 is lost again behind Z0, beyond that columns moved back shorten that stretch; why e13 is slow; and how much of e19's gain would hold in more runs.
